# Sixteen-token tiles with two buffers, all products on VectorE, and one queue for each direction

## The chip, the cores and the metric

The kernel runs on one core of a Trainium2 chip. The metric is the device time of one execution in microseconds. Four runs of the kernel before gave 242.47, 245.21, 243.01 and 245.73 us, a median of 244.11. The profile shows one execution, taken by the hardware profiler.

## The reference

Every token's row of 512 numbers is copied twice, and each copy is multiplied by its own weight. The indices of the experts are an input that nothing reads.

```python
batch, seq, hidden, k = 16, 1024, 512, 2
x_expanded = x[:, :, np.newaxis, :].repeat(k, axis=2)
weights = expert_weights[..., np.newaxis]
return (x_expanded * weights).astype(np.float32)
```

So 33.6 MB of x (float32) and 0.13 MB of weights are read, and 67.1 MB are written: `out[token, kk, :] = x[token, :] * w[token, kk]`.

## The kernel before, in words

The 16,384 tokens are cut into 128 runs of 128 consecutive tokens, one run for each partition. A partition's part of x is therefore 256 KB in one piece of memory, and its part of the output 512 KB in one piece. `w_tile` holds all weights, 256 for each partition; one transfer on SP's queue (L44) brings them in at the start.

The work goes in 16 iterations of 8 tokens for each partition. For each iteration `issue_load` takes one of three x tiles (16 KB per partition) and issues two loads of 4 tokens on ScalarE's queue (L53 and L54, 1 MB each, 8 KB in one piece for each partition). Loads 0 and 1 are issued ahead of the loop, and iteration `it` issues the loads of `it + 2` ahead of its own products. Those loads stand in ScalarE's instruction stream between the products of one iteration and the next.

Each iteration has two halves of 4 tokens. A half takes one of six output tiles (4 tokens x 2 copies x 512, 16 KB per partition), makes 8 products of 128 x 512, and stores the tile with one transfer on SP's queue (L93, 2 MB, 16 KB in one piece for each partition). In the first half all 8 products are on ScalarE (`nc.scalar.mul`, L79). In the second half the product with `opc` 0 is on VectorE and that with `opc` 4 on GpSimd (`tensor_scalar`, L85); the other six are on ScalarE. Since `opc` runs from 0 to 7, the case `opc == 8` never comes.

The order on each engine is that of the program; the framework adds the waits. A product waits until the load of its half has landed, and until the store that last read its output tile is done. A store waits for the eight products of its tile. A load waits until the products that read its x tile are done. Per partition the tiles take 3 x 16 + 6 x 16 + 1 = 145 KB.

Of the kernel before, what the change touches and what calls it, by code (L numbers as in the profile page):

```python
# [1 line left out]

# [4 lines left out]


@with_exitstack
def kernel(  # L10
    ctx: ExitStack,
    tc: tile.TileContext,
    x: bass.AP,
    expert_indices: bass.AP,
    expert_weights: bass.AP,
    out: bass.AP,
):
    nc = tc.nc

    batch, seq, hidden = x.shape  # L20
    k = expert_weights.shape[-1]
    P = nc.NUM_PARTITIONS
    ntok = batch * seq
    assert ntok % P == 0
    A_TOTAL = ntok // P

    xr = x.rearrange("b s h -> (b s) h").rearrange("(p a) h -> p a h", a=A_TOTAL)
    outr = out.rearrange("b s k h -> (b s) (k h)").rearrange(
        "(p a) n -> p a n", a=A_TOTAL
    )  # L30
    wr = expert_weights.rearrange("b s k -> (b s) k").rearrange(
        "(p a) k -> p a k", a=A_TOTAL
    )

    A = 8
    H = A // 2
    n_iters = A_TOTAL // A

    w_pool = ctx.enter_context(tc.tile_pool(name="w_pool", bufs=1))
    x_pool = ctx.enter_context(tc.tile_pool(name="x_pool", bufs=3))  # L40
    o_pool = ctx.enter_context(tc.tile_pool(name="o_pool", bufs=6))

    w_tile = w_pool.tile([P, A_TOTAL, k], mybir.dt.float32)
    nc.sync.dma_start(out=w_tile, in_=wr)  # L44

    x_tiles = {}

    def issue_load(j):
        if j >= n_iters:
            return  # L50
        t = x_pool.tile([P, A, hidden], mybir.dt.float32)
        a0 = j * A
        nc.scalar.dma_start(out=t[:, 0:H, :], in_=xr[:, a0 : a0 + H, :])  # L53
        nc.scalar.dma_start(out=t[:, H:A, :], in_=xr[:, a0 + H : a0 + A, :])  # L54
        x_tiles[j] = t

    issue_load(0)
    issue_load(1)

    for it in range(n_iters):  # L60
        a0 = it * A
        issue_load(it + 2)
        x_tile = x_tiles.pop(it)

        for half in range(2):
            o_tile = o_pool.tile([P, H, k, hidden], mybir.dt.float32)
            base = half * H
            opc = 0
            for ai in range(base, base + H):
                for kk in range(k):  # L70
                    w_ap = w_tile[:, a0 + ai, kk : kk + 1]
                    eng = nc.scalar
                    if half == 1:
                        if opc == 0 or opc == 8:
                            eng = nc.vector
                        elif opc == 4:
                            eng = nc.gpsimd
                    if eng is nc.scalar:
                        nc.scalar.mul(  # L79
                            out=o_tile[:, ai - base, kk, :],  # L80
                            in_=x_tile[:, ai, :],
                            mul=w_ap,
                        )
                    else:
                        eng.tensor_scalar(  # L85
                            out=o_tile[:, ai - base, kk, :],
                            in0=x_tile[:, ai, :],
                            scalar1=w_ap,
                            scalar2=None,
                            op0=mybir.AluOpType.mult,  # L90
                        )
                    opc += 1
            nc.sync.dma_start(  # L93
                out=outr[:, a0 + base : a0 + base + H, :], in_=o_tile
            )


# [1 line left out]
_INS = ['x', 'expert_indices', 'expert_weights']  # L99
_OUTS = [((16, 1024, 2, 512), 'float32')]  # L100


# [23 lines left out]
```

## Time and profile before

| | us |
|---|---|
| median of four runs | 244.11 |
| lowest and highest run | 242.47 and 245.73 |
| the profiled execution | 242.47 |
| its span, first to last instruction | 240.4 |
| ScalarE busy, 224 products and a table load | 140.2 |
| GpSimd busy, 16 products (1.846 each) among it | 29.7 |
| VectorE busy, 16 products (0.491 each) | 7.9 |
| the transfers: 32 stores of 2 MB, 32 loads of 1 MB, the weights | 100.82 MB, mean 419 GB/s |
| a store, from issue to landing (median) | 23.0 |
| a load, from issue to landing (median) | 28.1 |

The span runs from the first to the last instruction; the profiled execution's own time is 2.07 us longer. The profile cuts the span into 40 slices of 6 us: a digit is the busy share of an engine in tenths, `DMA` is the mean busy share of the 16 DMA engines, and `GB/s` what they moved. Queue q1 carries the transfers issued from SP (the stores and the weights), q10 those issued from ScalarE (the loads). In a line of a timeline stand the start, the duration, the engine, the line of the program, the operation with its tiles, the count, and the idle time before it with what ended it. In the stretches of time stand the busy time of VectorE, ScalarE and GpSimd, a clock that means nothing for this kernel, the busy share of the DMA engines, and their GB/s.

### The profile page before, as it was taken

To read this page: it belongs to the slowest core of one execution; us is meant where nothing else is said; L and a number is where in the kernel's file an instruction comes from. 1 tells how busy PE (TensorE), PEld (TensorE's weight loads), DVE (VectorE), ACT (ScalarE), POOL (GpSimd) and SP (SyncE) were. 2 spreads that over 40 slices of the span, in tenths; PEclk is the share of its full clock that TensorE was granted. 3 is DMA by queue.
4 is the path that set the end of the run, shared out by engine and by line. 5 is a ranking of instruction groups with operands and counts; after the bars stand their busy time and mean duration, and the time that the engine had idled before them with its cause. 6 is when DMAs were issued, how large, how long until landed. Compare 5 with 4: busy or idle time off the path is not lost.

```text
span 240.4 us, 500 instructions
## 1 busy us (share of the span) xinstructions
DVE 7.9 (3%) x16; ACT 140.2 (58%) x225; POOL 29.7 (12%) x20
## 2 busy tenths in 40 slices
DVE  0000000000000000000000000000000000000000
ACT  1989872928649094591936729277391897465000
POOL 0330303003020020301103020030300203002000
DMA  7999999999999999999999999999999999999995
GB/s 259 427 363 440 417 438 429 425 429 433 432 425 433 429 428 429 427 438 425 435 421 433 429 427 436 431 427 431 428 431 428 438 423 436 427 432 429 433 431 243
DMA packets 9363, 100.82 MB, mean 419 GB/s; under 512 B 1040, under 2 KB 1168, under 8 KB 1168
## 3 DMA queue, kind: packets, MB, share of 16 engines
q1 hardware_dynamic: 4752, 67.24, 65.5%
q10 hardware_dynamic: 4608, 33.56, 33.5%
q14 instruction: 3, 0.02, 0.0%
HBM read 33.69 MB, written 67.11 MB: 419 GB/s over the span
## 4 chain that ended last, share of the span: by engine, by line
DMA 83%; ACT 3%; ACTq 0%; issue 0%
DMA t<-in_x_dram 83%; ACT o_tile L79 3%; ACTq L121 0%; ACTq L79 0%
## 5 line engine op out<-in xcount | busy, mean ns | idle before, releaser
L79 ACT ACTIVATE o_tile<-t,w_tile 128x512 f32<-128x512 f32 x224 | 138.9, 706 | 74.6 <-DMA t<-in_x_dram 73.9
L85 POOL TENSOR_SCALAR o_tile<-t,w_tile 128x512 f32<-128x512 f32 x16 | 29.5, 1846 | 188.0 <-DMA t<-in_x_dram 188.0
L85 DVE TENSOR_SCALAR o_tile<-t,w_tile 128x512 f32<-128x512 f32 x16 | 7.9, 491 | 208.7 <-DMA t<-in_x_dram 208.7
L79 ACT ACT_TABLE_LOAD x1 | 1.3, 1283 | 5.0 <-DMA w_tile<-in_expert_weights_dram 5.0
L110 POOL MEMSET const-float32-0.0<- 128x1 f32 x1 | 0.1, 98 | 0.2 <-issue 0.2
L110 POOL MEMSET const-bfloat16-1.0<- 128x1 bf16 x1 | 0.1, 101 | 0.0
L110 POOL MEMSET const-uint8-127<- 128x1 uint8 x1 | 0.1, 101 | 0.0
L110 POOL MEMSET const-float32-1.0<- 128x1 f32 x1 | 0.1, 98 | 0.0
## 6 DMA issues: line engine op xcount, KB each, us to landing
out_dram<-o_tile SPq DMA_DIRECT2D x32, 2048.0 KB, 23.0
t<-in_x_dram ACTq DMA_DIRECT2D x32, 1024.0 KB, 28.1
w_tile<-in_expert_weights_dram SPq DMA_DIRECT2D x1, 128.0 KB, 4.2
```

What stands on the lines that cost most here:

```text
L79: nc.scalar.mul(out=o_tile[:, ai - base, kk, :], in_=x_tile[:, ai, :], mul=w_ap,)
L85: eng.tensor_scalar(out=o_tile[:, ai - base, kk, :], in0=x_tile[:, ai, :], scalar1=w_ap, scalar2=None, op0=mybir.AluOpType.mult,)
L110: nc = _bacc.Bacc("TRN2", target_bir_lowering=False, num_devices=1)
```

## The change

The mapping of tokens to partitions stays. There are now 8 tiles of 16 tokens. An x tile has 32 KB per partition, two buffers, and comes with one load of 4 MB on ScalarE's queue. An output tile has 64 KB per partition, two buffers, and leaves with one store of 8 MB on SP's queue, after its 32 products. All 256 products are on VectorE; ScalarE and GpSimd compute nothing. The loads are no longer issued ahead by the program: each stands in ScalarE's queue, which holds only loads, and waits there until its buffer is free. The tiles take 2 x 32 + 2 x 64 + 1 = 193 KB per partition.

The list `groups` could cut the tokens into groups, tiles and pieces; as set here there is one group of all 128 tokens, with eight tiles of one piece each. `TO` is 16, so `t % TO` is `t`, and a tile is stored once, at `t + 1 == 16`.

```diff
+    TX = 16
+    TO = 16
+    groups = [[[16], [16], [16], [16], [16], [16], [16], [16]]]
-    A = 8
-    H = A // 2
-    n_iters = A_TOTAL // A
...
-    x_pool = ctx.enter_context(tc.tile_pool(name="x_pool", bufs=3))
-    o_pool = ctx.enter_context(tc.tile_pool(name="o_pool", bufs=6))
+    x_pool = ctx.enter_context(tc.tile_pool(name="x_pool", bufs=2))
+    o_pool = ctx.enter_context(tc.tile_pool(name="o_pool", bufs=2))
...
+    def rows(of_all, done, T):
+        return of_all[done * P : (done + T) * P, :].rearrange(
+            "(p a) n -> p (a n)", a=T
+        )
...
+        for pieces in group:
+            x_tile = x_pool.tile([P, TX * hidden], f32)
+            at = 0
+            for n in pieces:
+                nc.scalar.dma_start(
+                    out=x_tile[:, at * hidden : (at + n) * hidden],
+                    in_=xr[:, (a0 + at) * hidden : (a0 + at + n) * hidden],
+                )
+                at += n
+            ends = [sum(pieces[: i + 1]) for i in range(len(pieces))]
+            first = 0
+            for t in range(at):
+                if t % TO == 0:
+                    o_tile = o_pool.tile([P, TO * row], f32)
                 for kk in range(k):
-                    w_ap = w_tile[:, a0 + ai, kk : kk + 1]
-                    eng = nc.scalar
-                    if half == 1:
-                        if opc == 0 or opc == 8:
-                            eng = nc.vector
-                        elif opc == 4:
-                            eng = nc.gpsimd
...
+                    nc.vector.tensor_scalar(
+                        out=o_tile[:, o : o + hidden],
+                        in0=x_tile[:, t * hidden : (t + 1) * hidden],
+                        scalar1=w_tile[:, c : c + 1],
+                        scalar2=None,
+                        op0=mybir.AluOpType.mult,
+                    )
+                if t + 1 in ends or (t + 1) % TO == 0:
+                    nc.sync.dma_start(
+                        out=outr[:, (a0 + first) * row : (a0 + t + 1) * row],
+                        in_=o_tile[:, first % TO * row : (t % TO + 1) * row],
+                    )
+                    first = t + 1
```

More of the change, by code (lines that the diff above doesn't have):

```diff
@@ L25 @@
     A_TOTAL = ntok // P
[L27 to L33, printed above, removed]
-    A = 8
-    H = A // 2
-    n_iters = A_TOTAL // A
-    w_pool = ctx.enter_context(tc.tile_pool(name="w_pool", bufs=1))
-    x_pool = ctx.enter_context(tc.tile_pool(name="x_pool", bufs=3))
@@ L41 @@
-    o_pool = ctx.enter_context(tc.tile_pool(name="o_pool", bufs=6))
[L43 to L69, printed above, removed]
-                for kk in range(k):
-                    w_ap = w_tile[:, a0 + ai, kk : kk + 1]
-                    eng = nc.scalar
-                    if half == 1:
-                        if opc == 0 or opc == 8:
-                            eng = nc.vector
-                        elif opc == 4:
-                            eng = nc.gpsimd
[L78 to L95, printed above, removed]
@@ new lines @@
+    f32 = mybir.dt.float32
+    row = k * hidden
+    TX = 16
+    TO = 16
+    groups = [[[16], [16], [16], [16], [16], [16], [16], [16]]]
+    assert sum(sum(sum(t) for t in g) for g in groups) == A_TOTAL
+    xf = x.rearrange("b s h -> (b s) h")
+    of = out.rearrange("b s k h -> (b s) (k h)")
+    wf = expert_weights.rearrange("b s k -> (b s) k")
+    w_pool = ctx.enter_context(tc.tile_pool(name="w_pool", bufs=1))
+    x_pool = ctx.enter_context(tc.tile_pool(name="x_pool", bufs=2))
+    o_pool = ctx.enter_context(tc.tile_pool(name="o_pool", bufs=2))
@@ new lines @@
+    w_tile = w_pool.tile([P, A_TOTAL * k], f32)
+    def rows(of_all, done, T):
+        return of_all[done * P : (done + T) * P, :].rearrange(
+            "(p a) n -> p (a n)", a=T
+        )
+    done = 0
+    for group in groups:
+        T = sum(sum(t) for t in group)
+        nc.sync.dma_start(
+            out=w_tile[:, done * k : (done + T) * k], in_=rows(wf, done, T)
+        )
+        done += T
+    done = 0
+    for group in groups:
+        T = sum(sum(t) for t in group)
+        xr = rows(xf, done, T)
+        outr = rows(of, done, T)
+        a0 = 0
+        for pieces in group:
[12 more added lines that the diff above has]
+                    o_tile = o_pool.tile([P, TO * row], f32)
+                for kk in range(k):
+                    c = (done + a0 + t) * k + kk
+                    o = t % TO * row + kk * hidden
+                    nc.vector.tensor_scalar(
[6 more added lines that the diff above has]
+                if t + 1 in ends or (t + 1) % TO == 0:
+                    nc.sync.dma_start(
+                        out=outr[:, (a0 + first) * row : (a0 + t + 1) * row],
+                        in_=o_tile[:, first % TO * row : (t % TO + 1) * row],
+                    )
+                    first = t + 1
+            a0 += at
+        done += T
```

## The prediction

> **What bounds the kernel now.** I read the page from the top: busy shares, then the 40 slices with the DMA queues, then the chain, and only then the groups of instructions.
>
> ```profile
> span 240.4 us, 500 instructions
> ...
> DVE 7.9 (3%) x16; ACT 140.2 (58%) x225; POOL 29.7 (12%) x20
> ...
> DMA  7999999999999999999999999999999999999995
> GB/s 259 427 363 440 417 438 429 425 429 433 432 425 433 429 428 429 427 438 425 435 421 433 429 427 436 431 427 431 428 431 428 438 423 436 427 432 429 433 431 243
> ...
> q1 hardware_dynamic: 4752, 67.24, 65.5%
> q10 hardware_dynamic: 4608, 33.56, 33.5%
> ...
> DMA t<-in_x_dram 83%; ACT o_tile L79 3%; ACTq L121 0%; ACTq L79 0%
> ```
>
> No engine is busy for more than 58% of the span, but the 16 DMA engines stand at 9 tenths in every slice but the first and the last, and the two queues' packets together take 99% of the span. The chain blames the loads for 83%, but a load is late only because stores share the same DMA engines. So the kernel is a transfer of 100.8 MB, and a change can do three things to it: alter the rate, put a hole into it, or alter its two ends. I therefore looked at stretches of time, for rate and holes:
>
> ```profile
> core 0: us, DVE busy (x) ACT busy (x) POOL busy (x), PEclk, DMA share, GB/s
> ...
> 8.00:12.00 4.00, 0.49 (x1) 4.00 (x8) 1.84 (x1) 1.00 1.01 428
> 12.00:16.00 4.00, 0.49 (x1) 3.54 (x6) 1.86 (x1) 1.00 1.00 332
> ...
> 84.00:114.00 30.00, 1.49 (x3) 17.82 (x29) 4.41 (x3) 1.00 1.01 430
> ...
> 226.00:230.00 4.00, 0.00 (x0) 0.00 (x0) 0.00 (x0) 1.00 1.02 438
> ```
>
> 8:12 is loads alone (428 GB/s), 84:114 both directions (430), 226:230 stores alone (438). The rate hardly depends on direction, and there is no hole. The one weak stretch is 12:16, where the first stores join queued loads: (428 - 332) x 4 / 430 = 0.9 us lost, once.
>
> For the products I need the pace of a run of instructions, and the trace of before has such a run only on ScalarE; VectorE's 16 products stand alone:
>
> ```profile
> 8.40 0.49 DVE L85 TENSOR_SCALAR o_tile<-t,w_tile 128x512 f32<-128x512 f32 x1 [8.40 <-DMA t<-in_x_dram]
> 13.30 0.49 DVE L85 TENSOR_SCALAR o_tile<-t,w_tile 128x512 f32<-128x512 f32 x1 [4.41 <-DMA t<-in_x_dram]
> ...
> 25.70 8.68 ACT L79 ACTIVATE o_tile<-t,w_tile 128x512 f32<-128x512 f32 x14 [0.74 <-DMA t<-in_x_dram]
> ```
>
> ScalarE's 14 products take 8.68 us; one alone takes 0.706, so they follow each other every (8.68 - 0.706) / 13 = 0.613 us and overlap by 0.093. The first two lines also date the loads: VectorE's product in each second half starts when that half has landed, so the second 1 MB of x was there at 8.4 and the fourth at 13.3.
>
> **The change, part by part.**
>
> *1. Products.* It removes 224 ScalarE products (138.9 us busy), 16 GpSimd products and the table load, and puts 256 on VectorE. One lasts 0.486 us at the median. No row shows two in a row. From above, the pace is bounded by no overlap: 0.486. From below I allow twice the overlap that ScalarE shows: 0.486 - 0.186 = 0.30. I take ScalarE's overlap, the nearest row: 0.486 - 0.093 = 0.393. The four 1-element MEMSETs of GpSimd support that order: 0.10 us each, yet started 0.03 apart, an overlap of 0.07. A tile of 16 tokens is 32 products: 31 x 0.393 + 0.486 = 12.7 us (9.8 to 15.6). All 256 are about 101 us, against 100.8 MB / 430.6 GB/s = 234 us of transfers; only where nothing is in flight do they show.
>
> [...]
>
> *2. The start: a new hole.* Now the first products wait for one load of 4 MB, not for 1 MB. Loads 0 and 1 are issued at once (two buffers), nothing else can be: load 2 needs the buffer that the products of tile 0 still read, and store 0 needs all 32 products. Step by step, on the clock of before:
> - load 0 is the same four MB that had landed at 13.3; products from 13.2 (fewer packets, 0.1).
> - Its packets ended some 0.5 earlier (the trace's packet records end at 12.8 for the fourth half), and load 1 follows at the pace of 8.4 to 13.3 (4.9 us for 2 MB): 9.7 us. DMA is empty from 12.7 + 9.7 = 22.4.
> - products end at 13.2 + 12.7 = 25.9. Store 0 (SP's queue, behind nothing but the weights) and load 2 (ACT's queue, which holds nothing else now) are issued then. The first load was issued at 0.72 and its first packet began at 1.9, so data flows again 1.1 to 1.2 later: 27.05.
> - hole: 27.05 - 22.4 = 4.65 us, wholly on the path, since the end is set by the transfers. Bounds by pace: 0.30 gives 1.75, 0.486 gives 7.5. Before, store 0 was issued at 11.28 with loads still queued, so this hole wasn't there.
>
> *3. Larger packets.* Rows per partition go from 8 to 32 KB (loads) and 16 to 64 KB (stores). The packet records have 309 ns for 8 KB and 611 for 16 KB: 302 ns for each 8 KB and 7 over. But packets overlap a little: in the steady part VectorE's starts are one iteration, 14.61 us, apart, and in that time each DMA engine moves 16 packets of either size, so a pair takes 14.61 / 16 = 0.913 us, only 7 ns over 3 x 302. Each DMA engine moves 256 pairs; three quarters of the overhead goes: 256 x 7 x 0.75 = 1.35 us. Taken: -1.35. Ends: 2.7 gained (7 ns on each packet), nothing if 64 KB is cut up again. On the loss side, nothing in the rows shows larger packets slower (611 is below twice 309); only at the end the DMA engines can finish apart by a packet, 4 x 0.61 instead of 0.61 us: 0 to +1.8, taken 0, since all have equal work.
>
> [...]
>
> *4. First stores.* The 0.9 us lost at 12:16 came as stores joined queued loads. Now store 0 and load 2 start on idle DMA engines. Ends 0 and -0.9; with nothing nearer to either, I take the middle, -0.45.
>
> *5. Steady part.* Products of tile i wait for load i and for store i-2 (two output buffers). While they run, store i-1 and load i+1 are queued: 12.6 MB, 29 us at 430 GB/s. Against it stand 0.5 + 12.7 + 1.1 = 14.3 us (17.2 at worst). Cost 0; the cover is 12 us wide. Behind the waiting store on SP stand only later stores, behind the waiting load on ACT only later loads; neither queue computes any more. Since packets of the two queues alternate one by one in the trace's byte shares (2:1, as their sizes), load i+2 and store i end together, which leaves the cover whole.
>
> *6. The end.* For tile 7 no load is left; its products have only store 6 as cover: 8.4 MB, 19.4 us, against 14.3 (17.2). Store 7 follows on without a hole: 0. What follows the last packets, 1.4 us without traffic (239.0 to 240.4), stays. GpSimd's share and the table load were off the path (ScalarE waited 5.0 us for weights first): 0. The weights' load is unchanged.
>
> **Sum:** +4.65 - 1.35 - 0.45 = +2.85 us. The profiled execution took 242.47 with a span of 240.4, so it would be 243.3 of span and 245.3. It was the fastest of the four runs; their median is 244.11. The hole is the same whichever run it is put into, so I add it to the median: 247.0.
>
> **The rivals.**
> - *VectorE overlaps more* (pace 0.30 to 0.35): hole 1.75 to 3.3, net about 0 to +1.5, time 244.8. For it: MEMSETs overlap most of their length. Against: ScalarE's row.
> - *VectorE overlaps not at all* (0.486): hole 7.5, net +5.7, time 249.8. From a pace of (19.4 - 1.6) / 32 = 0.556 on, a second hole opens before store 7; the longest single product is 0.512, so that is unlikely.
> - *Faster: large packets lift the rate itself.* The best long stretch of before is 438 GB/s. At that rate everywhere 234 us shrink by 234 x (1 - 430.6 / 438) = 4.0 us, which takes the place of the 1.35: net +4.65 - 4.0 - 0.45 = +0.2 and 244.3. From 443 GB/s on it is over 1% faster (4.65 - 6.65 - 0.45 = -2.45). Against: 8 KB and 16 KB packets run at nearly one rate (428 against 433 in the last 18 us of stores), so size has little left to give.
> - *The change doesn't make the hole:* if store 0's wait were covered by load 1, pace under about 0.25, the time is 242.3. It would need two and a half times ScalarE's overlap.
>
> **How the numbers follow.** Forecast 0.40 (own range 245.5 to 248.5, 0.27 of it above the 1% line at 246.55); more overlap 0.25; no overlap or a slower end 0.20; higher rate 0.08; no hole 0.07. About 1% is what a measurement of this kernel can tell from no change. Slower: 0.27 + 0.20 = 0.47. Faster: 0.10, most of the higher rate (0.06) and part of no hole (0.04). Same: the rest, 0.43. Range: all low ends, 1.75 - 2.7 - 0.9 = -1.85, give 242.3; the high end 7.5 with nothing gained gives 251.6. I take 242.5 to 251.5.
>
> **What would show it.** DMA slices with one dent near 22 to 27 us and none later; VectorE's first 32 products in 12.7 us; about 2,450 packets instead of 9,363; interior 433 GB/s; the first store issued near 25.9. Wrong would be: dents at every tile (then cover fails, step 5), a dent before the last store (step 6), an interior rate clearly off 430 (step 3), or 32 products in under 10 us.

## The result and the profile after

The changed kernel takes 248.27 us (median of 12 runs, 247.99 to 250.83). The kernel before has a median of 245.21 us over 17 runs (242.47 to 248.91), the four of above among them, so the medians lie 3.1 us apart. The ratio is 1.0208 (95% interval 1.0162 to 1.0253), or 5.1 us: like every ratio below it compares mean times (249.16 and 244.09 us here) and leaves out runs more than 1.5% above the fastest of the same kernel, five of the 17 here. The prediction said 247.0 us, range 242.5 to 251.5, and held "slower" to be the likeliest case at 0.47. The direction held, and so did the hole at the start; the other terms of the sum did not come out as forecast.

The page of the changed kernel, the same parts as were shown of before:

```profile
span 248.8 us, 337 instructions
...
DVE 102.0 (41%) x256; POOL 0.2 (0%) x4
...
DVE  0089992003970049600792019900397002970000
...
DMA  7994799899899989998998999899999999999990
GB/s 283 444 448 195 237 439 411 390 464 453 364 406 469 458 374 432 453 421 379 453 506 379 406 479 428 385 437 495 395 395 458 443 390 469 411 443 421 432 443 21
DMA packets 2450, 100.81 MB, mean 405 GB/s; under 512 B 272, under 2 KB 400, under 8 KB 400
...
q1 hardware_dynamic: 1296, 67.24, 63.2%
q10 hardware_dynamic: 1152, 33.55, 32.0%
```

The DMA row has one dent, the 4 in the fourth slice, while VectorE's row stands at 9 there: transfers wait for products. Later slices stay at 8 and 9, so no dent returns at each tile. The GB/s scatter more than before, partly because a packet of 64 KB lasts 2.4 us and the view books it as a whole. There are 2,450 packets instead of 9,363, as the prediction had counted.

The same kernel in stretches of time, first around the dent, then between the dent and the end, then at the end:

```profile
core 0: us, DVE busy (x) POOL busy (x), PEclk, DMA share, GB/s
20.00:22.00 2.00, 2.00 (x7) 0.00 (x0) 1.00 0.65 279
22.00:24.00 2.00, 2.00 (x7) 0.00 (x0) 1.00 0.00 0
24.00:26.00 2.00, 2.00 (x7) 0.00 (x0) 1.00 0.00 0
26.00:28.00 2.00, 2.00 (x6) 0.00 (x0) 1.00 1.38 524
28.00:30.00 2.00, 2.00 (x6) 0.00 (x0) 1.00 0.09 16
30.00:32.00 2.00, 2.00 (x6) 0.00 (x0) 1.00 1.12 279
36.00:226.00 190.00, 79.60 (x200) 0.00 (x0) 1.00 1.00 430
...
240.00:242.00 2.00, 0.00 (x0) 0.00 (x0) 1.00 0.98 426
242.00:244.00 2.00, 0.00 (x0) 0.00 (x0) 1.00 0.30 131
244.00:246.00 2.00, 0.00 (x0) 0.00 (x0) 1.00 0.08 33
```

The packets of load 1 end between 22.1 and 22.9 us, and nothing moves from there to 27.24: the hole. The 524 behind it is sixteen 64 KB packets booked where they begin. At the other end the DMA engines trail off over 5 us. The kernel before stopped within 2 us:

```profile
core 0: us, DVE busy (x) ACT busy (x) POOL busy (x), PEclk, DMA share, GB/s
236.00:238.00 2.00, 0.00 (x0) 0.00 (x0) 0.00 (x0) 1.00 0.82 352
238.00:240.40 2.40, 0.00 (x0) 0.00 (x0) 0.00 (x0) 1.00 0.03 14
```

VectorE's runs of products in the changed kernel, and the stores on SP's queue:

```profile
13.62 25.42 DVE L83 TENSOR_SCALAR o_tile<-x_tile,w_tile 128x512 f32<-128x512 f32 x64 [13.62 <-DMA x_tile<-in_x_dram]
60.22 12.76 DVE L83 TENSOR_SCALAR o_tile<-x_tile,w_tile 128x512 f32<-128x512 f32 x32 [21.18 <-DMA x_tile<-in_x_dram]
90.61 12.76 DVE L83 TENSOR_SCALAR o_tile<-x_tile,w_tile 128x512 f32<-128x512 f32 x32 [17.62 <-DMA x_tile<-in_x_dram]
...
26.41 196.31 SPq L91 DMA_DIRECT2D out_dram<-o_tile  x8
```

A tile's 32 products take 12.76 us (12.7 forecast), the first store is issued at 26.41 us (25.9 forecast), and before each later tile VectorE waits 16 to 21 us for transfers: it is no bound.

To see where the rest went, I summed the trace's packet records per DMA engine (means of the 16). "Packets" is the count of each size times its usual duration, less the overlap of neighbours; "lengthened" is what packets lasted beyond that; "idle" is time with fewer than 16 packets in flight: up to 4 us (start), from 4 to 226 us (middle) and from 226 us on (end). The columns add up to the end of the last packet.

```
us per DMA engine    packets lengthened idle start  idle middle  idle at end  last packet ends
before                 234.7     1.2       2.0          0.2          0.9         239.0
changed                232.5     3.8       2.0          5.8          3.5         247.7
changed, again (e7)    232.6     2.8       2.3          5.8          1.8         245.3
```

Against before: packets -2.2, lengthened +2.6, hole +5.7, ragged end +2.6, in all +8.7 for these two executions. That is more than the ratio says, since the one of before was the fastest of its first four runs and that of the changed kernel lies in the upper part of its own. Seven of its runs are at 247.99 to 248.33, five at 250.05 to 250.83. The step between them is about one 64 KB packet (2.418 us). In the profiled execution (250.55) one DMA engine began its last packet at 245.24, when the fifteen others had ended; in the other one (248.28, e7) the DMA engines end between 241.4 and 245.3. The cause of the two groups is not shown by this.

### The profile page after: what moved, and what is told of

The parts are those of the page before. It is cut to its first block, busy times and chain, and to the rows that moved or that the text cites. A ratio compares the mean times of both kernels' runs of the same rounds, so it can differ in the third digit from the quotient of the medians.

```text
span 248.8 us, 337 instructions
## 1 busy us (share of the span) xinstructions
DVE 102.0 (41%) x256; POOL 0.2 (0%) x4
## 2 busy tenths in 40 slices
DMA packets 2450, 100.81 MB, mean 405 GB/s; under 512 B 272, under 2 KB 400, under 8 KB 400
## 4 chain that ended last, share of the span: by engine, by line
DMA 56%; DVE 25%; another core or an unknown queue 7%; DVEq 0%; issue 0%
DMA x_tile<-in_x_dram 56%; DVE o_tile L83 25%; DVEq L123 0%; DVEq L83 0%
## 5 line engine op out<-in xcount | busy, mean ns | idle before, releaser
L83 DVE TENSOR_SCALAR o_tile<-x_tile,w_tile 128x512 f32<-128x512 f32 x256 | 102.0, 482 | 120.4 <-DMA x_tile<-in_x_dram 120.4
```

What stands on the lines that cost most here:

```text
L83: nc.vector.tensor_scalar(out=o_tile[:, o : o + hidden], in0=x_tile[:, t * hidden : (t + 1) * hidden], scalar1=w_tile[:, c : c + 1], scala ...
```

## The experiments

Two theories were set against each other. **A**: the hole before the first store carries the loss. **B**: the large packets carry it, through lengthened packets and DMA engines that end apart. Each ratio below is to the kernel before on the same chip.

**e1_two_engines.** Takes the hole away and leaves every transfer as it is (load 1 is also issued ahead of tile 0's products, which would else hold it up in ScalarE's queue; that part is left out here):

```diff
+                    if i == 0 and (t * k + kk) % 8 in (1, 4, 7):
+                        nc.scalar.mul(...)       # 12 of tile 0's 32 products
+                    else:
                         nc.vector.tensor_scalar(
```

> The changed kernel with one edit: of the 32 products of tile 0, 12 go to ScalarE beside 20 on VectorE, so that the first store can be issued at about 21.8 us instead of 26.4; every transfer keeps its size and its packets, and the other 224 products stay on VectorE. Theory A (the hole before the first store carries most of the loss): the hole shrinks from 5.1 us to 0.7 to 1.0 and the time falls by 4 to 4.5 us against the changed kernel, to a ratio of about 1.003 against the kernel before. Theory B (the large packets carry it: longer packets, a first store that stalls, and one DMA engine that ends a packet of 2.4 us late): the hole closes as well, but the time falls by less than 2 us and stays 1% or more above the kernel before.

Measured: 245.99 us, ratio 1.0136 (1.0123 to 1.0149). Stretches of this kernel around the first store:

```profile
core 0: us, DVE busy (x) ACT busy (x) POOL busy (x), PEclk, DMA share, GB/s
20.00:22.00 2.00, 1.97 (x5) 1.43 (x3) 0.00 (x0) 1.00 0.99 426
22.00:24.00 2.00, 0.33 (x1) 0.00 (x0) 0.00 (x0) 1.00 1.44 541
24.00:26.00 2.00, 2.00 (x6) 0.00 (x0) 0.00 (x0) 1.00 0.23 49
26.00:28.00 2.00, 2.00 (x6) 0.00 (x0) 0.00 (x0) 1.00 0.95 295
```

Most of the hole is gone (idle in the middle 1.25 us per DMA engine instead of 5.8). The time falls by 4.3 us against the median of e7 below (250.26 us on another chip, where the kernel before also took 242.7 us), and by 4.6 and 2.4 us between the profiled executions (245.92 against 250.55 and 248.28). But 1.4% remains: lengthened packets stay at 4.1 us, the end at 2.3 us. Neither theory is enough.

**e3_first_in_pieces.** Tile 0 alone is loaded and stored in four pieces:

```diff
-    groups = [[[16], [16], [16], [16], [16], [16], [16], [16]]]
+    groups = [[[4, 4, 4, 4], [16], [16], [16], [16], [16], [16], [16]]]
```

> The changed kernel with one edit: tile 0 alone is loaded in four transfers of 1 MB and stored in four of 2 MB, each as soon as its 8 products are done; tiles 1 to 7 are as in the changed kernel. The first store is issued near 9 to 10 us, while loads are still queued. Theory A: no hole, time 4.5 to 5 us under the changed kernel, ratio about 1.000 to 1.003. Theory B: ratio 1.01 or more, with the late end still there.

Measured: 246.37 us, ratio 1.0151 (1.0120 to 1.0182), idle in the middle 0.14, lengthened 5.3, end 3.1. Theory A alone fails a second time: no hole, and still 1.5%.

**e2_small_packets.** Loads and stores in transfers of 1 and 2 MB, with products ordered to keep the hole:

```diff
+            for b in range(0, TX, 4):          # four loads of 4 tokens
+                nc.scalar.dma_start(...)
...
+            for t in [b + r for r in (3, 2, 1, 0) for b in (12, 8, 4, 0)]:
...
+            for b in range(0, TX, 4):          # four stores of 4 tokens
+                nc.sync.dma_start(...)
```

> The changed kernel with its tiles, buffers and hole, but every load in four transfers of 1 MB (8 KB rows) and every store in four of 2 MB (16 KB rows); the products of a tile are ordered so that all four stores become ready only at its end. Theory A: the hole of about 5 us stays and the 1.4 us of packet overhead come back, so the time is the same as the changed kernel's or up to 1.5 us longer, ratio 1.02 to 1.027 against the kernel before. Theory B: the late DMA engine and the lengthened packets go, the time falls by 3 to 4 us, ratio about 1.005 to 1.01.

Measured: 244.44 us, ratio 1.0068 (1.0056 to 1.0080). It doesn't tell what it was made for: tile 0's products did not run in the order of the program, but began with the first piece (at 5.98 us), the first store was issued at 9.26 us, and the hole was gone too (idle in the middle 0.12).

**e5_padded** and **e6_padded_two_engines** repair that. Padding breaks the rows, so packets are 8 and 16 KB in the same eight loads and eight stores (8,595 packets on e5's page and 8,594 on e6's, against 2,450); e6 adds the edit of e1.

```diff
-            x_tile = x_pool.tile([P, TX * hidden], f32)
+            x_tile = x_pool.tile([P, TX // 4, 4 * hidden + 16], f32)
...
-                    o_tile = o_pool.tile([P, TO * row], f32)
+                    o_tile = o_pool.tile([P, TO // 4, 4 * row + 16], f32)
```

> The changed kernel with one edit: 64 bytes of padding behind every fourth token in the x and output tiles, so that a load of 4 MB goes in 8 KB packets and a store of 8 MB in 16 KB packets. Tiles, transfers, waits and the hole of about 5 us before the first store are those of the changed kernel. Theory A' (hole and large packets both cost): the hole stays, 1.5 us of packet overhead come back, but the end at which DMA engines finish up to a packet apart shrinks from 3 to 5 us to about 1.5 and the lengthened packets go: 1 to 3 us faster than the changed kernel, ratio to the kernel before about 1.015. Theory B' (only the hole costs): 1.5 us slower than the changed kernel. Theory C (only the packets cost): ratio 1.005 or less.

> The padded kernel with 12 of tile 0's 32 products on ScalarE, so small packets and no hole, but still tiles of 16 tokens and two buffers. Theory A': 4 us under the padded kernel, ratio to the kernel before about 1.000 to 1.004. If it stays at 1.01 or more, something else in the change costs: the two large buffers or the pace of the products.

**e7_after_again** is the changed kernel on the same chip.

> The changed kernel unaltered, on the same chip as the three others of this call, so that its two clusters of times (about 248.1 and 250.6) can be set beside them. All theories: ratio 1.02, and where a profile falls on the upper cluster, one DMA engine ends about 2.4 us after the others.

Measured: e5 251.38 us, 1.0368 (1.0342 to 1.0395); e6 244.05 us, 1.0061 (1.0043 to 1.0079); e7 250.26 us, 1.0295 (1.0254 to 1.0336). Together with e1:

```
ratio to before      hole              no hole
64 and 32 KB packets 1.0208 and 1.0295 1.0136 (e1)
16 and 8 KB packets  1.0368 (e5)       1.0061 (e6)
```

The hole costs with either packets. With small packets its idle time is plain on e5's page:

```profile
DMA  7996599999999999999999999999999999999995
GB/s 240 426 429 285 208 394 431 425 418 429 429 434 411 429 426 431 422 434 427 426 430 425 426 434 427 429 419 435 431 427 423 429 438 422 435 433 427 435 430 220
```

Apart from the dent, the DMA row is nearly that of before, and the spans of the two profiled executions, 247.0 (e5) and 242.0 (e6), differ by 5.0 us, nearly the difference of the idle time in the middle (5.1 - 0.35 us per DMA engine). In these runs large packets help beside a hole (1.0295 against 1.0368, one chip) and hurt without one (1.0136 against 1.0061, two chips; lengthened 4.1 us against 2.0). The second comparison is the weaker one: e1 still has 0.9 us more idle time in the middle than e6, and the same changed kernel came out at 1.0208 and 1.0295 in two sets of runs, mostly because the kernel before took 244.09 us in one and 242.7 in the other. So theory B' is right about e5 and wrong about e1, theory A' is wrong about e5 and, with 1.0061 against at most 1.004, nearly right about e6; that the sign of the packet term depends on the hole is likely, not shown. e5's runs go from 248.75 (the profiled one) to 252.43, and what the slower ones add to the idle time was not seen in a profile.

**e12_longer_hole.** The opposite dose: e1 with all of tile 0's products on ScalarE.

```diff
-                    if i == 0 and (t * k + kk) % 8 in (1, 4, 7):
+                    if i == 0 and (t * k + kk) % 8 >= 0:
```

> The changed kernel with all 32 products of tile 0 on ScalarE, 19.7 us instead of 12.8, so that the first store is issued at about 33.3 us: the hole grows from 5.1 to about 12 us and nothing else changes. If the hole lies wholly on the path, the time grows by 7 us against the changed kernel, to 255 to 258; if part of it is made up later, by less.

Measured: 259.82 us, 1.0710 (1.0696 to 1.0723). The first store was issued at 36.12 us, not 33.3, when VectorE had also finished tile 1 (why it waited for that is not shown): 9.7 us later than in the changed kernel. The time is 9.6 us longer than e7's (9.2 and 11.4 us between the profiled executions), and the mean idle time in the middle grows from 5.8 to 15.2 us. The page shows the hole as a slice with 0:

```profile
DMA  7993048999999999899989999899989999989992
GB/s 304 433 422 163 0 163 295 447 437 447 396 407 438 432 468 407 381 437 473 442 386 437 437 468 437 366 401 462 457 376 433 417 457 412 488 376 437 488 396 112
```

So the hole lies on the path at full price; nothing later makes it up.

**e4_vector_only.** The other part of the change alone: the kernel before with all products on VectorE.

```diff
-                    eng = nc.scalar
-                    if half == 1: ...
+                    eng = nc.vector
```

> The kernel before with one edit: all products on VectorE, tiles, buffers, loads and stores as they were. The loads of an iteration no longer stand behind products in ScalarE's queue. Both theories: 8 products take 3.3 us against 7.3 us of transfers, all hidden, so within 0.5% of the kernel before; if moving the products costs or gains by itself, it shows here: over 1% either way would contradict the sum, which put the move at nothing outside the hole.

Measured: 244.67 us, ratio 1.0090 (1.0054 to 1.0126): a miss. With transfers of the same sizes, lengthened packets go from 1.2 to 3.2 us, the idle time at the end from 0.9 to 3.0, and the last DMA engine ends at 242.95 instead of 239.01. Stretches of this kernel:

```profile
84.00:87.00 3.00, 0.25 (x1) 0.00 (x0) 1.00 0.96 404
87.00:92.00 5.00, 3.01 (x8) 0.00 (x0) 1.00 1.02 362
92.00:97.00 5.00, 0.00 (x0) 0.00 (x0) 1.00 1.01 433
```

The packet records show why 87 to 92 is weak: from 85.5 to 90.6 us only loads ran, and just ahead of the stores' return 54 load packets begun within 3.6 us lasted over 350 ns instead of 309, 0.8 us in all per DMA engine. It looks the same as at the first stores of before, at 12 to 16 us. A weaker one (0.2 us) lies near 61 us.

**e8_scalar_only, e9_scalar_vector_spare, e10_vector_scalar_spare** ask whether VectorE's work or the pace of the queues does this. e8 puts all products of before on ScalarE, e9 adds VectorE work that nothing uses, e10 is e4 with unused work on ScalarE.

```diff
-                    if half == 1: ...                    # all three; eng stays nc.scalar in e8 and e9
+                    nc.vector.tensor_scalar(out=spare, ...)   # e9
...
+                    eng = nc.vector                      # e10
+                    nc.scalar.mul(out=spare, ...)             # e10
```

> The kernel before with all products on ScalarE, at 0.613 us each 4.9 us for the 8 of a half against 7.3 us of transfers. It asks why the kernel with all products on VectorE was 0.9% slower. Theory P (pace of the loads: with ScalarE's queue free, loads run ahead, stores run dry in the middle, and each time stores rejoin a stretch of loads alone about 0.8 us are lost on all DMA engines): loads stay behind products as before, one such event at the start, ratio within 0.3% of the kernel before. Theory V (leaving the mix of three engines costs by itself): 0.5% or more slower, as with VectorE alone.

> The kernel with all products on ScalarE (0.998 of the kernel before), and beside it VectorE makes each product a second time into two spare buffers that nothing stores: work added on VectorE, transfers and ScalarE's queue unchanged. Theory V (VectorE's products lengthen packets): 1 to 2 us of lengthened packets after 34 us as in the kernel with all products on VectorE, ratio 1.005 or more. Theory P (only the order and pace of loads and stores matters): ratio within 0.2% of 0.998, lengthened packets after 34 us under 0.2 us per DMA engine.

> The kernel with all products on VectorE (1.009 of the kernel before), and beside it ScalarE makes each product a second time into two spare buffers that nothing stores, so that the loads stand behind products in ScalarE's queue again, as in the kernel before. Theory P: the loads are paced, no stretch of loads alone in the middle, ratio 0.997 to 1.002. Theory V: stays at 1.005 or more.

Measured: e8 242.17 us, 0.9980 (0.9970 to 0.9991); e9 242.79 us, 1.0012 (0.9992 to 1.0033); e10 245.89 us, 1.0126 (1.0096 to 1.0156). In e9 VectorE is busy for 103.9 us and packets after 34 us are lengthened by 0.14 us per DMA engine, against 1.9 in e4: theory V falls as far as e9 can tell, though e9's ratio, 0.3% above e8's, is also over what theory P allowed (0.2%). And theory P fails in e10: the loads stand behind products again and there is no burst of long packets (0.6 us after 34 us), yet two DMA engines end at 241.6 and 242.3 us, the other fourteen by 239.4. What puts single DMA engines behind when VectorE makes the stored products is open. e8, the only kernel under before, has this page:

```profile
DMA  7999999999999999999999999999999999999996
GB/s 258 425 361 431 428 436 428 428 432 434 427 425 439 423 432 427 434 431 429 427 436 435 420 438 423 425 431 436 421 436 432 431 429 424 435 431 435 427 435 295
```

It has no dent, and its idle time at the end is 0.4 us per DMA engine. It beats both kernels, by 0.2% over before.

**e11_double_tiles.** e8 with iterations of 16 tokens:

```diff
-    A = 8
+    A = 16
-    o_pool = ctx.enter_context(tc.tile_pool(name="o_pool", bufs=6))
+    o_pool = ctx.enter_context(tc.tile_pool(name="o_pool", bufs=3))
```

> The kernel with all products on ScalarE, with iterations of 16 tokens (loads of 2 MB in 16 KB packets, stores of 4 MB in 32 KB packets, three x tiles of 32 KB and three output tiles of 32 KB per partition). The first store needs a load of 2 MB and 16 products and is issued near 19 us, while 12 MB of loads are queued for 29 us: no hole. If larger packets save their overhead where loads are paced: 0.9 us less, ratio about 0.994. If larger packets bring lengthened packets and a ragged end by themselves: ratio 1.003 or more.

Measured: six runs from 249.93 to 256.30 us (median 253.75), ratio 1.0346 (1.0310 to 1.0382), although its first store met queued loads. Stretches of the execution of 249.93 us:

```profile
212.00:216.00 4.00, 4.00 (x8) 0.00 (x0) 1.00 1.00 434
216.00:220.00 4.00, 4.00 (x8) 0.00 (x0) 1.00 0.67 287
220.00:236.00 16.00, 8.60 (x15) 0.00 (x0) 1.00 0.99 426
236.00:240.00 4.00, 0.00 (x0) 0.00 (x0) 1.00 0.69 295
240.00:244.00 4.00, 0.00 (x0) 0.00 (x0) 1.00 0.13 57
244.00:248.00 4.00, 0.00 (x0) 0.00 (x0) 1.00 0.04 16
```

Three DMA engines had fallen behind: of the transfers that end near 208 us thirteen DMA engines had reported their part by 201 us, the last one only at 208.8. With three output tiles the products waited for that (ScalarE goes on at 208.91, after 5.24 us of waiting for a store), the next stores came late, and from 217.5 us on thirteen DMA engines stood empty for up to 2.6 us. In the end thirteen finish at 239.3, two at 242.6 and one at 247.0: the ragged end, 6.8 us of idle time per DMA engine, is the largest cost of this kernel.

## Why the prediction was right, and where its sizes were off

1. *Products.* Right. The pace is (12.76 - 0.482) / 31 = 0.396 us, against 0.393 taken from ScalarE's overlap: on average a product started 0.086 us before the one ahead had ended (0.482 - 0.396), between the bounds of no overlap (0.486) and twice ScalarE's (0.30). That the products show "only where nothing is in flight" is not confirmed: e4 loses 0.9% by their move alone, with transfers of the same sizes.
2. *The hole.* Right in mechanism, and priced at full cost by e12. DMA was empty from 22.2 (one DMA engine from 22.9) instead of 22.4, and data came at 27.25 instead of 27.05; with a pause of some DMA engines between their first store and first load, near 30 us, the mean idle time rises by 5.7 us instead of 4.65.
3. *Larger packets.* The overhead was saved, even 2.2 us instead of 1.35. Two things ate it. The step said that "nothing in the rows shows larger packets slower": lengthened packets cost 2.6 more in one profiled execution and 1.6 in the other (e7). And "the DMA engines can finish apart by a packet, 4 x 0.61 instead of 0.61 us: 0 to +1.8, taken 0, since all have equal work" was the term that was mis-sized most: +2.6 and +0.9. The interior rate is the 430 GB/s of before (36 to 226 us), not the 433 forecast.
4. *First stores.* Taken as -0.45, and nothing was gained. Packets begun from 27 to 45 us are lengthened by 1.4 us per DMA engine, against the 0.9 us of before at its first stores; even the first sixteen store packets, which began on idle DMA engines, lasted 2.76 us on average instead of 2.418.
5. *Steady part.* Right: no dent from tile to tile; VectorE waits 16 to 21 us for transfers ahead of each later tile.
6. *The end.* The cover before store 7 held for thirteen DMA engines; it was issued at 222.4 us, and three waited for it 0.7 to 1.2 us from 222.1 on. What follows the last packets stayed, 1.1 us (247.7 to 248.8) against 1.4; the ragged end ahead of them is the error of step 3 again.

*The time.* That 247.0 lies only 1.3 us under the measured median is in part luck. From profiled execution to profiled execution the sum forecast +2.85 us, and +8.1 (250.55) and +5.8 (248.28, e7) were measured over 242.47: the hole was 1.0 us larger, and steps 3 and 4, forecast at -1.8, came to +3.0 and +0.4 by the packet records. The forecast was added to a median of 244.11, 1.6 us above that execution; beside e1 to e12 the kernel before took about 242.7. A sum that was too small thus met a base higher than most later runs of before; why before took longer in its first runs is not shown.

Against the rivals: no overlap and more overlap are both out by the pace; that large packets lift the rate by themselves is out by the interior 430 GB/s, e1 and e11; that no hole opens is out by the stretch of 0 GB/s.

## What to carry to other kernels

When transfers are the bound, ask of a larger tile when its first store can be issued and whether enough loads are queued until then; the empty time was paid in full here (5 to 6 us, and 9.4 more when it was stretched). Count too how far apart the DMA engines can end: in the changed kernel fifteen had ended by 245.24 us and the last at 247.66, and with the three output tiles of e11 the products waited 5.24 us for the slowest one. Moving work between two engines that are both far from busy was not free here either: e4 (VectorE at 43%) lies 0.9% over before and e8 (ScalarE at 67%) 0.2% under. Why is not shown; the order in which loads are issued does not explain it, since e10 puts them behind products again and still lies 1.3% over.

## What the runs showed that was not expected

- Just ahead of stores that join a stretch of loads alone, load packets of 8 KB lasted up to 776 ns (at 13 to 16 us of before) and 840 ns (at 87 to 91 us of e4) instead of 309, 0.8 to 0.9 us in all per DMA engine.
- Apart from hole, start and end, the DMA engines were hardly idle in the steady part of e4, e10 or the changed kernel (about 0.1 us per DMA engine from 34 to 216 us), so an engine that ends late is slowed, not starved. In e10 all 49 packets that were lengthened by over 20 ns between 45 and 216 us belong to stores, and they come a few at a time, about once for each store (every 7.3 to 7.5 us). The cause is open.
- The changed kernel's first twelve runs fall into two groups about 2.4 us apart, the duration of one 64 KB packet; of e7's six runs one (249.81) lies between them.
